# Attention scores of two maps, or of two heads, side by side in the upper and lower half of TensorE's array

## The chip, the cores and the metric

The kernel runs on one core of one Trainium2 chip. The metric is device time in microseconds (us) of one execution; of several runs the median counts. Durations of single instructions come from one profiled execution of the kernel, taken by the hardware profiler.

## The reference

An encoder trunk of two layers over 1024 tokens of width 1024, in float32. Each layer has a token mixer and an MLP with squared ReLU, both followed by a LayerNorm of the scaled residual. The mixer runs three groups beside each other: a convolution, differential attention (4 heads, with two score maps of 64 channels each) and attention to a memory of 256 rows (4 heads of 64 channels). What the change touches is this:

```python
# differential attention, per block of 128 queries and per head (dh = 64, S = 1024)
s1 = jnp.einsum("bhqd,bhkd->bhqk", q1b, k1).astype(jnp.float32) * scale + bias
s2 = jnp.einsum("bhqd,bhkd->bhqk", q2b, k2).astype(jnp.float32) * scale + bias
attn = jax.nn.softmax(s1, axis=-1) - lam * jax.nn.softmax(s2, axis=-1)
return jnp.einsum("bhqk,bhkd->bhqd", attn.astype(vh.dtype), vh)
...
# attention to the memory (MEM_DH = 64, 256 keys)
s = jnp.einsum("bshd,bmhd->bhsm", qh, km).astype(jnp.float32) * (MEM_DH ** -0.5)
p = jax.nn.softmax(s, axis=-1).astype(vm.dtype)
return jnp.einsum("bhsm,bmhd->bshd", p, vm).reshape(B, S, MEM_W)
```

## The kernel before

All large products run on TensorE in a float32 format of its own (`F32R` in the code). To keep precision each operand is split into a high and a low part (`split`), and a product is made of several: high x high, high x low and low x high, which is what `mm3` issues (L115 to L117).

A layer goes through stages: the input projection (`in_proj`, products `pj`, `v_ps`), the attention stage (`attention`), the output projection (`wo_ps`) with a LayerNorm, the MLP's upper product (`uz`, `uc`, `ud`) and its lower product (`db`, `dz`). The attention stage takes the heads in the order 0, memory (called head 4), 1, 2, 3, each in 8 blocks of 128 queries. A block passes through four steps in a software pipeline (`pipeline`):

- `scores`: TensorE makes the scores in PSUM; VectorE adds the bias, reduces to the row's extreme and writes to SBUF (L541); ScalarE takes the exponential (L543). For the memory it is a maximum (L551) and four exponentials (L555).
- `combine`: VectorE joins the two maps (L561 to L563), or the rows of the memory's heads are divided by their sums.
- `turn`: TensorE transposes the block (`at`, L199, 8 products of 128 columns), and it is split again by ScalarE with VectorE or with TensorE (L209).
- `values`: the products with the values (`o`, 24 of 256 columns for two blocks; `mo` for the memory), then the norm's small products (`ms`, L621 and L634).

A score has only 64 channels to sum over, and the array has 128 rows. For the differential heads the kernel stacks the high part of the queries on the low part (`qs`, 128 rows) and keeps the keys' high and low part twice, once in each half of the rows (`ks`, four slots). So a map of 128 queries by 512 keys takes two products of 128 rows (L538 with the keys' high parts, L539 with their low parts), and a block takes 8. For the memory two heads lie in the 128 rows of `qm`, and the keys `km` hold zeros where a row belongs to the other head, so one `mm3` makes both.

Scores go to a pool of two buffers of two PSUM banks each (`psum2`), one buffer per map. The memory's keys take the place of head 0's keys (`heads["k"]`, one buffer), and the load of a next head starts when the head before it begins (`before`, `load`). The order of the instructions on each engine is not the program's: a scheduler sorts them by priority when the program is built, and every engine then keeps that order.

Of the kernel before, what the change touches and what calls it, by code (L numbers as in the profile page):

```python
# [2 lines left out]

# [1 line left out]

# [7 lines left out]
F32R = mybir.dt.float32r  # L13
# [6 lines left out]
P = 128  # L20
T = 1024
# [4 lines left out]
MEM = 256  # L26
# [28 lines left out]
def encoder(ctx: ExitStack, tc: tile.TileContext, x, memt, w_f, w_v, w_mk, w_mv, w_out, w_up,  # L55
            w_down, par, lamv, bvr, emb_g, emb_b, rel, onehot, b_out, ln1_g, ln1_b, ln2_g, ln2_b, out):
    nc = tc.nc
# [6 lines left out]
    big = pool("big")  # L64
# [9 lines left out]
    def f(ap):  # L74
        return ap.bitcast(F32)
# [14 lines left out]
    def psum2(name):  # L90
        return pa.tile([P, 2, 512], F32, tag="pa", name=name)
# [14 lines left out]
    def weight(src, name, wpool=None, tag="w8", bufs=3, lo=None, hi=None):  # L106
        raw = wts.tile([P, 1024], F32, tag="raw", name=f"{name}_raw", bufs=3)
        loads.append(nc.sync.dma_start(raw, src))
        w = (wpool or wts).tile([P, 2, 1024], F32R, tag=tag, name=name, bufs=bufs)
        split(w[:, 0], w[:, 1], raw, lo or nc.gpsimd, hi)  # L110
        return w

    def mm3(ps, lhs, rhs, start, stop):

        nc.tensor.matmul(ps, lhsT=lhs[0], rhs=rhs[0], start=start, stop=False)  # L115
        nc.tensor.matmul(ps, lhsT=lhs[0], rhs=rhs[1], start=False, stop=False)  # L116
        nc.tensor.matmul(ps, lhsT=lhs[1], rhs=rhs[0], start=False, stop=stop)  # L117
# [367 lines left out]

    def attn_load(l, h, qd, kd, bt, qs, ks):
        nc.sync.dma_start(bt, skew[h][0:P * 2048].rearrange("(p n) -> p n", n=2048)[:, P - 1:P - 1 + BTW])
        for m in range(2):
            src = slice(64 * m, 64 * m + 64)
            for half in range(2):  # L490
                dst = slice(64 * half, 64 * half + 64)
                nc.sync.dma_start(f(ks[dst, 2 * m:2 * m + 2]), kd[src])
                nc.sync.dma_start(f(qs[dst, m]), qd[src, half])
        return ks, qs, bt

    def attention(l, heads, load, qmd, kvd, vt, lam, mixd, right):
# [10 lines left out]

        def out_w(kc, pr=None):
            wos[kc] = weight(w_out[l, kc * P:(kc + 1) * P, :], f"wo{l}_{kc}", *((pr, "wc", 5) if pr else ()), lo=nc.vector if kc in (4, 7) else None, hi=nc.gpsimd if kc in (1, 3, 5) else None)

        def scores(k):

            h, qb = k["h"], k["qb"]
            nm = f"{l}_{h}_{qb}"
            nonlocal ns
            if h == 0 and qb < 2:
                sc = wts.tile([P, 2, T], F32, tag="w8", name=f"s{nm}", bufs=3)
            elif h == NH and qb % 2:
                sc = k["prev"]["sc"][:, 1:2]
            elif ns % 3 == 0 and (h != NH - 1 or qb > 1):  # L520
                sc = heads["s"].tile([P, 2, T], F32, tag="s", name=f"s{nm}", bufs=1)
                ns += 1
            else:
                ns += 1
                sc = heads["b"].tile([P, 2, T], F32, tag="s", name=f"s{nm}", bufs=2)
            k["sc"] = sc
            if qb % 4 == 0 or (h == NH and qb % 2 == 0):
                sts[h, qb // 4] = sm.tile([P, 4, 8], F32, tag="ast", name=f"ast{nm}", bufs=3)
            st = k["st"] = sts[h, qb // 4][:, qb % 4]
            q = slice(qb * P, (qb + 1) * P)  # L530
            if h < NH:
                ks, qs, bt = heads[h]
                b0 = T - P - qb * P
                for m in range(2):
                    ps = psum2(f"sc{nm}_{m}")
                    for hf in range(2):
                        cs = slice(hf * 512, hf * 512 + 512)
                        nc.tensor.matmul(ps[:, hf], lhsT=qs[:, m, q], rhs=ks[:, 2 * m, cs], start=True, stop=False)  # L538
                        nc.tensor.matmul(ps[:, hf], lhsT=qs[:, m, q], rhs=ks[:, 2 * m + 1, cs], start=False, stop=True)  # L539

                    nc.vector.tensor_tensor_reduce(out=sc[:, m], in0=ps.rearrange("p a b -> p (a b)"), in1=bt[:, b0:b0 + T], scale=-0.125,  # L541
                                                   scalar=3e38, op0=ALU.add, op1=ALU.min, accum_out=st[:, m:m + 1])
                    nc.scalar.activation(sc[:, m], sc[:, m], AF.Exp, scale=-1.0, bias=st[:, m:m + 1], accum_out=st[:, 2 + m:3 + m])  # L543
            else:
                qm, km = heads[h], heads["km"]
                ps = psum2(f"sc{nm}")
                pv = ps.rearrange("p a (b m) -> p (a b) m", b=2)
                for c in range(2):
                    hs = slice(2 * c, 2 * c + 2)
                    mm3(ps[:, c], (qm[c][:, 0, q], qm[c][:, 1, q]), (km[:, 0, hs], km[:, 1, hs]), True, True)  # L550
                nc.vector.tensor_reduce(out=st[:, 0:4], in_=pv, op=ALU.max, axis=AX.X)  # L551
                nc.vector.tensor_scalar_mul(st[:, 0:4], st[:, 0:4], -0.125)
                p = sc[:, 0].rearrange("p (h m) -> p h m", h=NH)
                for i in range(NH):
                    nc.scalar.activation(p[:, i], pv[:, i], AF.Exp, scale=0.125, bias=st[:, i:i + 1], accum_out=st[:, 4 + i:5 + i])  # L555
# [32 lines left out]
        def values(k):  # L588

            h, qb, at = k["h"], k["qb"], k["at"]  # L590
            if h == NH:
                qc, vz = qb // 2, heads["vz"]
                pq = psum1(f"mo{l}_{qc}")
                for c in range(2):
                    for j in range(4):
                        i, mb = 2 * c + j // 2, j % 2
                        mm3(pq[:, 256 * c:256 * c + 256], (vz[:, 0, mb, i], vz[:, 1, mb, i]), (at[:, 0, 2 * i + mb], at[:, 1, 2 * i + mb]),
                            j == 0, j == 3)
                mx = wts.tile([P, 1024], F32, tag="raw", name=f"mmx{l}_{qc}", bufs=3)[:, 0:512]
                nc.scalar.activation(mx, pq, AF.Copy)  # L600
                for c in range(2):
                    store_mix(mx[:, 256 * c:256 * c + 256], mixd, 6 + c, 2 * qc, 2)
                return
# [4 lines left out]
            pq = po[h, qq]  # L608
# [125 lines left out]
    for l in range(L):  # L734
# [10 lines left out]
        def load(h):  # L745

            if h == 0:
                heads["k"] = heads["s"] = pool(f"k{l}", es=right, side="right")
            pr = heads["pool", h % 2]
            bt = pr.tile([P, BTW], F32, tag="bt", name=f"bt{l}_{h}", bufs=1)  # L750
            qs = pr.tile([P, 2, T], F32R, tag="qs", name=f"qs{l}_{h}", bufs=1)
            if h:
                ks = big.tile([P, 4, T], F32R, tag="b16", name=f"ks{l}_{h}", bufs=4)
            else:
                ks = heads["k"].tile([P, 4, T], F32R, tag="ks", name=f"ks{l}_{h}", bufs=1)
            heads[h] = attn_load(l, h, qd[h], kd[h], bt, qs, ks)

        heads["pool", 0] = pool(f"h{l}_0", es=right, side="right")
# [443 lines left out]
```

## Time and profile before

| | |
|---|---|
| median of 3 runs | 2441.92 us (2439.93 to 2450.11) |
| profiled execution | 2442.68 us |
| its span in the profile | 2440.8 us |
| granted TensorE clock, mean over the span | 0.987 |
| TensorE busy | 2320.9 us, 95% of the span |
| VectorE busy | 1769.6 us, 73% |
| ScalarE busy | 1174.7 us, 48% |

A busy time is the time in which at least one instruction of the engine is under way; matmuls overlap, so TensorE's busy time is not time at full rate. The attention stage lies at about 272 to 507 us in layer 0 and 1478 to 1701 us in layer 1. Names such as `sc<-ks,qs` say what is written and read, buffer numbers left out.

### The profile page before, as it was taken

The numbers are of one execution on the slowest core, as the hardware profiler recorded it, in microseconds if no ns is written. First come the engines' busy times: TensorE is split into PE (matmuls) and PEld (weight loads), VectorE is DVE, ScalarE is ACT, GpSimd is POOL, SyncE is SP. The second block draws the span as 40 slices with busy tenths as digits, with TensorE's granted clock in tenths as the row PEclk, the third lists the DMA queues.
The fourth block names the chain that finished last, engine by engine and source line by source line (L and its number), as shares of the span: only waits on it lengthen the run. The fifth ranks groups of instructions, "written<-read, shape, count | busy, mean of one in ns | idle before, by whom it ended". The sixth has DMA issues, their size and how long they took to land.

```text
span 2440.8 us, 30655 instructions
## 1 busy us (share of the span) xinstructions
PE 2320.9 (95%) x11516; PEld 1937.3 (79%) x11516; DVE 1769.6 (73%) x2516; ACT 1174.7 (48%) x2034; POOL 273.9 (11%) x184
## 2 busy tenths in 40 slices
PE   5999999999999998999999999999999999899997
PEld 4888788787788886888878887887878888688886
DVE  8697868847666657667789967786676566586768
ACT  5212488844655554333432227975465455433332
POOL 2224021111000000000033411111100000000002
PEclk9999999999999999999999999999999999999999
DMA  8252545241344458343332436434324444944332
GB/s 317 84 197 87 185 120 146 72 173 70 125 160 151 155 203 343 105 164 95 112 118 87 131 103 201 105 85 146 116 95 139 161 145 158 351 168 167 100 95 95
DMA packets 137740, 355.76 MB, mean 146 GB/s; under 512 B 14804, under 2 KB 31956, under 8 KB 130900
## 3 DMA queue, kind: packets, MB, share of 16 engines
q1 hardware_dynamic: 137592, 353.81, 43.3%
q8 instruction: 90, 1.47, 0.2%
q14 instruction: 58, 0.48, 0.1%
HBM read 240.47 MB, written 117.47 MB: 147 GB/s over the span
## 4 chain that ended last, share of the span: by engine, by line
PE 77%; DVE 16%; ACT 3%; DMA 3%; issue 2%; SPq 0%; DVEq 0%; ACTq 0%
PE uz L873 14%; PE db L1054 14%; PE dz L1054 10%; PE uc L873 7%; DVE acc L347 7%; PE ud L873 4%; PE wo_ps L117 2%; PE wo_ps L116 2%; PE wo_ps L115 2%; PE at L199 2%; DVE s L541 2%; PE pj L115 2%; PE pj L117 2%; PE pj L116 2%; PE sc L538 1%
## 5 line engine op out<-in xcount | busy, mean ns | idle before, releaser
L1054 PE MATMUL db<-wf,hf 128*128 128x512 f32 x1536 | 357.6, 392 | 22.7 <-ACT hf L99 21.6
L1054 PEld LDWEIGHTS db<-wf,hf 128*128 128x128 f32 x1536 | 289.5, 189 | 85.3 <-ACT hf L99 22.4
L1054 PE MATMUL dz<-wf,hf 128*128 128x512 f32 x1152 | 263.6, 389 | 0.0
L102 DVE TENSOR_TENSOR wf<-wd,wf 128x1024 fp32r<-128x1024 f32 x112 | 138.7, 1238 | 161.6 <-ACT wf L99 159.4
L1054 PEld LDWEIGHTS dz<-wf,hf 128*128 128x128 f32 x1152 | 216.7, 188 | 45.1
L99 ACT ACTIVATE wf<-wd 128x1024 fp32r<-128x1024 f32 x112 | 118.1, 1056 | 272.9 <-PE db L1054 132.4
L99 ACT ACTIVATE wu<-wu_r 128x512 fp32r<-128x512 f32 (+1 forms) x192 | 131.8, 708 | 219.8 <-PE uc L873 96.5
L873 PE MATMUL uz<-x,wu 128*128 128x512 f32 x768 | 191.5, 395 | 0.0
L873 PE MATMUL uz<-xt,wu 128*128 128x512 f32 x768 | 185.7, 389 | 1.0 <-ACT wu L99 1.0
L347 DVE SCALAR_TENSOR_TENSOR acc<-u,pp,acc 128x1009 f32<-128x1009 f32 (+14 forms) x120 | 185.4, 1585 | 0.6
L115 PE MATMUL pj<-x_h,wf 128*128 128x512 f32 x448 | 175.3, 392 | 1.7 <-ACT x_h L99 1.7
L116 PE MATMUL pj<-x_l,wf 128*128 128x512 f32 x448 | 175.1, 391 | 1.6 <-DVE l_row L126 1.6
L117 PE MATMUL pj<-x_h,wf 128*128 128x512 f32 x448 | 174.6, 390 | 0.0
L102 DVE TENSOR_TENSOR wu<-wu_r,wu 128x512 fp32r<-128x512 f32 (+1 forms) x192 | 145.9, 777 | 37.0 <-ACT wu L99 36.5
L873 PEld LDWEIGHTS uz<-x,wu 128*128 128x128 f32 x768 | 146.2, 191 | 31.2 <-ACT p L884 0.4
L873 PEld LDWEIGHTS uz<-xt,wu 128*128 128x128 f32 x768 | 143.9, 188 | 31.6 <-ACT wu L99 1.6
L541 DVE CUSTOM_DVE_ANT_0 s<-sc,bt 128x1024 f32<-128x1024 f32 x128 | 152.9, 1217 | 22.0 <-PE sc L539 15.6
L166 POOL TENSOR_TENSOR yd<-yd,l2g 128x1024 f32<-128x1024 f32 x6 | 17.2, 2870 | 1294.9 <-ACT yd L165 1294.9
L99 ACT ACTIVATE hf<-hr 128x1024 fp32r<-128x1024 f32 x112 | 117.3, 1049 | 93.9 <-PE db L1054 41.1
L543 ACT ACTIVATE s<-s,ast 128x1024 f32<-128x1024 f32 x128 | 148.4, 1164 | 26.8 <-DVE ast L541 26.4
L890 DVE TENSOR_TENSOR h<-u,uc 128x512 f32<-128x512 f32 x64 | 44.0, 687 | 135.2 <-PE uc L873 114.7
L102 DVE TENSOR_TENSOR hf<-hr,hf 128x1024 fp32r<-128x1024 f32 x112 | 137.0, 1223 | 4.1 <-ACT hf L99 4.1
(261 smaller groups left out, 5082.8 us busy)
## 6 DMA issues: line engine op xcount, KB each, us to landing
hr<-hd SPq DMA_DIRECT2D x224, 256.0 KB, 2.9
wu_r<-in_w_up SPq DMA_DIRECT2D x64, 512.0 KB, 4.1
hd<-hs SPq DMA_DIRECT2D x128, 256.0 KB, 2.9
wd<-in_w_down SPq DMA_DIRECT2D x64, 512.0 KB, 7.3
hd<-h SPq DMA_DIRECT2D x96, 256.0 KB, 2.1
ks<-kd SPq DMA_DIRECT2D x32, 512.0 KB, 9.8
wf_raw<-in_w_f SPq DMA_DIRECT2D x28, 512.0 KB, 4.2
qd<-stg SPq DMA_DIRECT2D x8, 1024.0 KB, 4.3
```

The lines of the kernel that those rows point to most:

```text
L99: nc.scalar.activation(hi, src, AF.Copy)
L102: (lo_eng or nc.vector).tensor_tensor(lo, src, f(hi), op=ALU.subtract)
L115: nc.tensor.matmul(ps, lhsT=lhs[0], rhs=rhs[0], start=start, stop=False)
L116: nc.tensor.matmul(ps, lhsT=lhs[0], rhs=rhs[1], start=False, stop=False)
L117: nc.tensor.matmul(ps, lhsT=lhs[1], rhs=rhs[0], start=False, stop=stop)
L199: nc.tensor.matmul(pt[:, j * P:(j + 1) * P], lhsT=src, rhs=ident, start=j == 0, stop=j == 3, is_transpose=True, skip_group_check=True)
L347: nc.vector.scalar_tensor_tensor(acc[:, c, a:b], u[:, c, a + t - PAD:b + t - PAD], pp[:, k:k + 1], acc[:, c, a:b], ALU.mult, ALU.add)
L541: nc.vector.tensor_tensor_reduce(out=sc[:, m], in0=ps.rearrange("p a b -> p (a b)"), in1=bt[:, b0:b0 + T], scale=-0.125, scalar=3e38, op0= ...
L543: nc.scalar.activation(sc[:, m], sc[:, m], AF.Exp, scale=-1.0, bias=st[:, m:m + 1], accum_out=st[:, 2 + m:3 + m])
L873: nc.tensor.matmul(ps, lhsT=a[:, kc], rhs=x[:, c, kc], start=start and kc == 0 and n == 0, stop=stop and kc == 3 and n == 2, skip_group_ch ...
L890: nc.vector.tensor_tensor(h, a, ps, op=op)
L1054: nc.tensor.matmul(ps, lhsT=h[:, a, n, ts], rhs=w[c][:, n], start=start and n == 0 and m == 0, stop=stop and n == 1 and m == 2, skip_group ...
```

## The change

The scores of a head's two maps are now made side by side: map 0 in rows 0 to 63 of the array, map 1 in rows 64 to 127, in the places in which `qd` and `kd` hold them. A map takes three products of 64 rows (high x high, high x low, low x high) for each half of the keys, and the new function `halves` issues one of map 1 and one of map 0 in turn, into the two buffers of the block. It also ties each such product behind the one before it on TensorE, and gives all but the first of a block another priority in the scheduler. The memory's heads are made in pairs in the same way, with 256 columns each, and their order in the banks changes with it. Queries and keys are loaded with one transfer each.

```diff
@@ -1,5 +1,5 @@
 import math
-from contextlib import ExitStack
+from contextlib import ExitStack, nullcontext
 
 import numpy as np
 
@@ -485,12 +485,8 @@
 
     def attn_load(l, h, qd, kd, bt, qs, ks):
         nc.sync.dma_start(bt, skew[h][0:P * 2048].rearrange("(p n) -> p n", n=2048)[:, P - 1:P - 1 + BTW])
-        for m in range(2):
-            src = slice(64 * m, 64 * m + 64)
-            for half in range(2):
-                dst = slice(64 * half, 64 * half + 64)
-                nc.sync.dma_start(f(ks[dst, 2 * m:2 * m + 2]), kd[src])
-                nc.sync.dma_start(f(qs[dst, m]), qd[src, half])
+        nc.sync.dma_start(f(ks), kd)
+        nc.sync.dma_start(f(qs), qd)
         return ks, qs, bt
 
     def attention(l, heads, load, qmd, kvd, vt, lam, mixd, right):
@@ -507,6 +503,18 @@
 
         def out_w(kc, pr=None):
             wos[kc] = weight(w_out[l, kc * P:(kc + 1) * P, :], f"wo{l}_{kc}", *((pr, "wc", 5) if pr else ()), lo=nc.vector if kc in (4, 7) else None, hi=nc.gpsimd if kc in (1, 3, 5) else None)
+
+        pairs = []
+
+        def halves(outs, lhs, rhs, start=True, stop=True):
+
+            for n, (a, c) in enumerate(((0, 0), (0, 1), (1, 0))):
+                for m in (1, 0):
+                    r = slice(64 * m, 64 * m + 64)
+
+                    with (tc.issue_after(pairs[-1].ins) if pairs else nullcontext()), tc.high_priority(offset=0 if start and n == 0 and m else 400):
+                        pairs.append(nc.tensor.matmul(outs[m], lhsT=lhs[m][a][r], rhs=rhs[m][c][r], start=start and n == 0,
+                                                      stop=stop and n == 2, skip_group_check=True))
 
         def scores(k):
 
@@ -531,12 +539,11 @@
             if h < NH:
                 ks, qs, bt = heads[h]
                 b0 = T - P - qb * P
-                for m in range(2):
-                    ps = psum2(f"sc{nm}_{m}")
-                    for hf in range(2):
-                        cs = slice(hf * 512, hf * 512 + 512)
-                        nc.tensor.matmul(ps[:, hf], lhsT=qs[:, m, q], rhs=ks[:, 2 * m, cs], start=True, stop=False)
-                        nc.tensor.matmul(ps[:, hf], lhsT=qs[:, m, q], rhs=ks[:, 2 * m + 1, cs], start=False, stop=True)
+                pm = [psum2(f"sc{nm}_{m}") for m in range(2)]
+                for hf in range(2):
+                    cs = slice(hf * 512, hf * 512 + 512)
+                    halves([pm[m][:, hf] for m in range(2)], [(qs[:, 0, q], qs[:, 1, q])] * 2, [(ks[:, 0, cs], ks[:, 1, cs])] * 2)
+                for m, ps in enumerate(pm):
 
                     nc.vector.tensor_tensor_reduce(out=sc[:, m], in0=ps.rearrange("p a b -> p (a b)"), in1=bt[:, b0:b0 + T], scale=-0.125,
                                                    scalar=3e38, op0=ALU.add, op1=ALU.min, accum_out=st[:, m:m + 1])
@@ -545,9 +552,10 @@
                 qm, km = heads[h], heads["km"]
                 ps = psum2(f"sc{nm}")
                 pv = ps.rearrange("p a (b m) -> p (a b) m", b=2)
+
                 for c in range(2):
-                    hs = slice(2 * c, 2 * c + 2)
-                    mm3(ps[:, c], (qm[c][:, 0, q], qm[c][:, 1, q]), (km[:, 0, hs], km[:, 1, hs]), True, True)
+                    halves([ps[:, i, c * MEM:(c + 1) * MEM] for i in range(2)], [(qm[c][:, 0, q], qm[c][:, 1, q])] * 2,
+                           [(km[:, 0, 2 * c + i], km[:, 1, 2 * c + i]) for i in range(2)], c == 0, c == 1)
                 nc.vector.tensor_reduce(out=st[:, 0:4], in_=pv, op=ALU.max, axis=AX.X)
                 nc.vector.tensor_scalar_mul(st[:, 0:4], st[:, 0:4], -0.125)
                 p = sc[:, 0].rearrange("p (h m) -> p h m", h=NH)
@@ -593,8 +601,8 @@
                 pq = psum1(f"mo{l}_{qc}")
                 for c in range(2):
                     for j in range(4):
-                        i, mb = 2 * c + j // 2, j % 2
-                        mm3(pq[:, 256 * c:256 * c + 256], (vz[:, 0, mb, i], vz[:, 1, mb, i]), (at[:, 0, 2 * i + mb], at[:, 1, 2 * i + mb]),
+                        i, o, mb = 2 * c + j // 2, c + j // 2 * 2, j % 2
+                        mm3(pq[:, 256 * c:256 * c + 256], (vz[:, 0, mb, i], vz[:, 1, mb, i]), (at[:, 0, 2 * o + mb], at[:, 1, 2 * o + mb]),
                             j == 0, j == 3)
                 mx = wts.tile([P, 1024], F32, tag="raw", name=f"mmx{l}_{qc}", bufs=3)[:, 0:512]
                 nc.scalar.activation(mx, pq, AF.Copy)
@@ -750,9 +758,9 @@
             bt = pr.tile([P, BTW], F32, tag="bt", name=f"bt{l}_{h}", bufs=1)
             qs = pr.tile([P, 2, T], F32R, tag="qs", name=f"qs{l}_{h}", bufs=1)
             if h:
-                ks = big.tile([P, 4, T], F32R, tag="b16", name=f"ks{l}_{h}", bufs=4)
+                ks = big.tile([P, 4, T], F32R, tag="b16", name=f"ks{l}_{h}", bufs=4)[:, 0:2]
             else:
-                ks = heads["k"].tile([P, 4, T], F32R, tag="ks", name=f"ks{l}_{h}", bufs=1)
+                ks = heads["k"].tile([P, 4, T], F32R, tag="ks", name=f"ks{l}_{h}", bufs=1)[:, 0:2]
             heads[h] = attn_load(l, h, qd[h], kd[h], bt, qs, ks)
 
         heads["pool", 0] = pool(f"h{l}_0", es=right, side="right")
```

The first place is TensorE's order at block 3 of head 2. Before (`sc_2_3_0` and `sc_2_3_1` are the block's two maps):

```order
L538 MATMUL sc_2_3_0_3668<-ks_2_3063,qs_2_3062 128x512
L539 MATMUL sc_2_3_0_3668<-ks_2_3063,qs_2_3062 128x512
L538 MATMUL sc_2_3_0_3668<-ks_2_3063,qs_2_3062 128x512
L539 MATMUL sc_2_3_0_3668<-ks_2_3063,qs_2_3062 128x512
L538 MATMUL sc_2_3_1_3675<-ks_2_3063,qs_2_3062 128x512
L539 MATMUL sc_2_3_1_3675<-ks_2_3063,qs_2_3062 128x512
L538 MATMUL sc_2_3_1_3675<-ks_2_3063,qs_2_3062 128x512
L539 MATMUL sc_2_3_1_3675<-ks_2_3063,qs_2_3062 128x512
L199 MATMUL at_2_0_0_3567<-ident,s_2_0_3488 128x128 x4
```

Now, the last three pairs of the same block and what follows:

```order
L516 MATMUL sc_2_3_1_3769<-ks_2_3131,qs_2_3130 128x512
L516 MATMUL sc_2_3_0_3768<-ks_2_3131,qs_2_3130 128x512
L516 MATMUL sc_2_3_1_3769<-ks_2_3131,qs_2_3130 128x512
L516 MATMUL sc_2_3_0_3768<-ks_2_3131,qs_2_3130 128x512
L516 MATMUL sc_2_3_1_3769<-ks_2_3131,qs_2_3130 128x512
L516 MATMUL sc_2_3_0_3768<-ks_2_3131,qs_2_3130 128x512
L209 MATMUL at_2_1_0_3705<-at_2_0_3662,minus 128x512
L209 MATMUL at_2_1_1_3713<-at_2_0_3662,minus 128x512
```

The block's products stay together in both. There were four for map 0 and then four for map 1; now all twelve alternate between the maps, and both maps end with the last pair.

The second place is TensorE's order between head 0's last scores (`sc_0_7`) and the memory's first (`sc_4_0`). Before, the end of that piece:

```order
L116 MATMUL o_0_0_2467<-at_0_2_2416,v_6_671 128x256
L117 MATMUL o_0_0_2467<-at_0_2_2416,v_6_671 128x256
L115 MATMUL o_0_0_2467<-at_0_2_2416,v_7_672 128x256
L116 MATMUL o_0_0_2467<-at_0_2_2416,v_7_672 128x256
L117 MATMUL o_0_0_2467<-at_0_2_2416,v_7_672 128x256
L199 MATMUL at_0_5_1_2552<-ident,s_0_5_2492 128x128 x4
L209 MATMUL at_0_4_1_2518<-at_0_4_2510,minus 128x512
L209 MATMUL at_0_5_0_2544<-at_0_4_2510,minus 128x512
L621 MATMUL ms_0_0_2587<-ones,rms_0_2328 128x1 x4
```

Now, from the last pair of head 0 on:

```order
L516 MATMUL sc_0_7_1_2630<-ks_0_2044,qs_0_2043 128x512
L516 MATMUL sc_0_7_0_2629<-ks_0_2044,qs_0_2043 128x512
L209 MATMUL at_0_5_0_2566<-at_0_4_2528,minus 128x512
L209 MATMUL at_0_5_1_2574<-at_0_4_2528,minus 128x512
L629 MATMUL ms_0_0_2609<-ones,rms_0_2326 128x1 x4
L199 MATMUL at_0_6_0_2651<-ident,s_0_6_2544 128x128 x4
L199 MATMUL at_0_6_1_2658<-ident,s_0_6_2544 128x128 x4
L209 MATMUL at_0_6_1_2658<-at_0_6_2650,minus 128x512
L516 MATMUL sc_4_0_2674<-kv_2323,qm_2320 128x256 x12
```

Before, 11 value products of head 0 (`o`) and two groups of four transpositions (`at`, L199) stood in this piece. Now no value product stands here: they come after the memory's first scores, and eight transpositions and a third L209 fill the place.

The third place is the beginning of block 4 of head 1 now:

```order
L199 MATMUL at_1_2_1_3338<-ident,s_1_2_3241 128x128 x4
L516 MATMUL sc_1_4_1_3349<-ks_1_2668,qs_1_2667 128x512
L209 MATMUL at_1_2_1_3338<-at_1_2_3330,minus 128x512
L516 MATMUL sc_1_4_0_3348<-ks_1_2668,qs_1_2667 128x512
L516 MATMUL sc_1_4_1_3349<-ks_1_2668,qs_1_2667 128x512
L516 MATMUL sc_1_4_0_3348<-ks_1_2668,qs_1_2667 128x512
```

The first product of the block stands alone, with one of L209 behind it, and the others follow in turn. That is so for 30 blocks; in all, TensorE's order now has 106 stretches of paired products, with 960 products where there were 608.

## Rows read from the trace of the kernel before

**Rows 1.** The profile page, part 1: busy us (share of the span), instructions
```profile
PE 2320.9 (95%) x11516; PEld 1937.3 (79%) x11516; DVE 1769.6 (73%) x2516; ACT 1174.7 (48%) x2034; POOL 273.9 (11%) x184
```

**Rows 2.** Stretches: length, PE, PEld, DVE, ACT, POOL busy us, granted clock, DMA
```profile
272.00:507.00 235.00, 220.97 (x1353) 187.63 (x1352) 181.30 (x336) 181.74 (x379) 36.55 (x42) 0.97 0.43 122
1478.00:1701.00 223.00, 208.78 (x1315) 180.28 (x1314) 166.42 (x315) 172.92 (x365) 38.84 (x43) 0.98 0.44 123
```

**Rows 3.** Chain of waits inside the same two stretches, shares
```profile
by line: PE at L199 10.6%; DVE s L541 9.5%; PE sc L538 7.9%; PE sc L539 7.3%; PE o L115 5.6%; PE o L116 5.5%; PE o L117 5.5%; PE at L209 4.2%; DVE s L563 3.2%; issue 3.1%; ACT s L555 3.0%; PE ms L634 2.3%; ACT at L208 2.2%; DMA kv<-kvd 2.0%
...
by line: PE at L199 11.4%; DVE s L541 9.5%; PE sc L538 7.8%; PE sc L539 7.4%; PE o L115 6.6%; PE o L116 6.5%; PE o L117 6.5%; PE at L209 4.5%; DVE s L563 3.5%; PE ms L634 2.8%; DMA kv<-kvd 2.2%; issue 2.2%; PE wo_ps L116 2.1%; PE wo_ps L115
```

**Rows 4.** Groups by line and shape, TensorE: count, busy us, mean ns, idle
```profile
L538 PE MATMUL sc<-ks,qs 128*128 128x512 f32 x256 | 108.6, 424 | 14.8 <-DVE ast L541 13.0 <-PE sc L539 0.9 <-ACT s L555 0.4
L539 PE MATMUL sc<-ks,qs 128*128 128x512 f32 x256 | 103.1, 403 | 0.0
...
L115 PE MATMUL sc<-kv,qm 128*128 128x512 f32 x32 | 14.3, 447 | 3.1 <-DMA kv<-kvd 1.6 <-ACT s L555 1.4
...
L116 PE MATMUL sc<-kv,qm 128*128 128x512 f32 x32 | 13.1, 410 | 0.0
```

**Rows 5.** Timeline of TensorE, a block of head 1: start us, length us, instruction
```profile
372.47 0.39 PE L538 MATMUL sc<-ks,qs 128*128 128x512 f32 x1
372.70 0.39 PE L539 MATMUL sc<-ks,qs 128*128 128x512 f32 x1
372.92 0.39 PE L538 MATMUL sc<-ks,qs 128*128 128x512 f32 x1
373.15 0.39 PE L539 MATMUL sc<-ks,qs 128*128 128x512 f32 x1
373.38 1.91 PE L199 MATMUL at<-ident,s 128*128 128x128 f32 x16
```

**Rows 6.** Timeline of TensorE, transpositions and then value products
```profile
308.02 1.09 PE L199 MATMUL at<-ident,s 128*128 128x128 f32 x8
308.87 0.37 PE L115 MATMUL o<-at,v 128*128 128x256 f32 x1
309.07 0.28 PE L116 MATMUL o<-at,v 128*128 128x256 f32 x1
309.19 0.28 PE L117 MATMUL o<-at,v 128*128 128x256 f32 x1
```

**Rows 7.** Busy time by stretch, around the memory's scores of layer 0
```profile
316.00:326.00 10.00, 8.80 (x46) 7.23 (x45) 6.92 (x17) 5.92 (x13) 0.00 (x0) 0.83 0.82 295
340.00:360.00 20.00, 19.15 (x123) 16.06 (x122) 10.27 (x23) 18.41 (x59) 9.28 (x20) 1.00 0.13 38
```

**Rows 8.** Who waited for the products that read ks (us, times)
```profile
who waited for it (us, times):
  DVE s L541: 15.6, 15
```

**Rows 9.** The profile page, part 5: the reduction of a map's scores
```profile
L541 DVE CUSTOM_DVE_ANT_0 s<-sc,bt 128x1024 f32<-128x1024 f32 x128 | 152.9, 1217 | 22.0 <-PE sc L539 15.6
```

**Rows 10.** Chain of waits in order of time, layer 0 (start us, us)
```profile
316.74 4.75 DMA kv<-kvd
```

**Rows 11.** Timeline of TensorE, up to the memory's first scores
```profile
320.28 1.05 PE L621 MATMUL ms<-ones,rms 128*128 128x1 f32 x8 [0.91 <-ACT om L618]
321.62 0.76 PE L115 MATMUL sc<-kv,qm 128*128 128x512 f32 x1 [0.29 <-DMA kv<-kvd]
322.19 0.63 PE L116 MATMUL sc<-kv,qm 128*128 128x512 f32 x1
322.61 0.63 PE L117 MATMUL sc<-kv,qm 128*128 128x512 f32 x1
```

**Rows 12.** The profile page, part 6: KB each, us from issue to landing
```profile
ks<-kd SPq DMA_DIRECT2D x32, 512.0 KB, 9.8
```

**Rows 13.** Timeline of TensorE's weight loads, same block of head 1
```profile
376.05 0.19 PEld L539 LDWEIGHTS sc<-ks,qs 128*128 128x128 f32 x1
```

## The prediction

> **What bounds the kernel now.** I read the engines' totals first. TensorE holds matmuls for 95% of the span, VectorE and ScalarE much less [rows 1]. The change touches only the attention stage of each layer, so the rest is read there. In the two stretches that hold it, 235 and 223 us long, TensorE is busy 221 and 209 us, VectorE 181 and 166, ScalarE 182 and 173 [rows 2]: TensorE leads, the other two are not far behind. The chain of waits inside those stretches says the same in shares: the score products (L538 and L539) hold 15.2% of it in both layers, that is 35.7 and 33.9 us, VectorE's reduction of the scores (L541) another 9.5% [rows 3]. So score products count when they get shorter, but not all of them.
>
> How many are there? 256 and 256 of 512 columns for the four differential heads, and 3 x 32 for the memory's heads (L115 to L117, the third is like the second) [rows 4]. Their listed length (about 0.4 us) is not their price, for they overlap. The price is the distance between starts: 372.47, 372.70, 372.92, 373.15, 373.38, so 0.2275 us [rows 5]. That makes 512 x 0.2275 = 116.5 us for the heads (58.2 per layer) and 96 x 0.2275 = 21.8 us for the memory. Of the 116.5 us the chain holds 35.7 + 33.9 = 69.6, a share of 0.6. I take this 0.6 as what the end feels of a microsecond of TensorE there.
>
> **The scores of the heads.** Before, a block (128 queries of one head) issues 8 products of 128 rows: two maps, two halves of the keys, two products. Now it issues 12 of 64 rows, always one of map 1 and then one of map 0. No product of 64 rows with such a partner is in the trace, so a pair is bounded: at best it takes the time of one product, 0.2275 us; at worst its two run in turn, 0.455 us. Each product also has its own weight load. The nearest row for their rate are the transpositions, where load and product come in turn with 128 columns each: 8 from 308.02 to 308.87, 0.106 us each [rows 6]. Two loads take 0.21 us and still fit beneath 0.2275. I take full overlap: the two halves of a pair read different partitions and write different banks, and nothing in a row speaks against it. Then 2 layers x 4 heads x 8 blocks = 64 blocks, x 6 pairs = 384 pairs x 0.2275 = 87.4 us, 29.1 less than 116.5. With the share of 0.6: -17.5 us. The point from which it turns: 8 x 0.2275 = 6 pairs x 0.303, so a pair must stay under 0.303 us.
>
> The Trainium skill, page "TensorE: Matmul & The Clock Gate", Part 3 (packing small matmuls), gives 3.07 times for four products of 32 rows side by side, and a model by which partners start 4 ns apart. No run here shows it yet. An estimate from that 3.07 of a possible 4 would give a pair 0.2275 x 2 / 1.53 = 0.297 us, 114 us in all, and hardly any gain; from the 4 ns it would be the 87.4 above.
>
> **The memory's scores.** 96 products of 512 columns become 96 pairs of 256. A product of 256 columns starts 0.12 us after the one before [rows 6], so 11.4 us at best; at the rate of two loads per pair (0.21) 20.2 us; in turn (0.24) 23. That is -10 to +1 against 21.8. I take the loads' rate, being the nearest row, with some of it overlapped: -5 on TensorE, and -3 at the end, since ScalarE holds 18.4 of 20 us in that part [rows 7].
>
> **What is added.** A block's two maps used to be finished one after the other: VectorE could begin after 4 products (0.91 us) while TensorE made the second map. Now both end together after 6 pairs, 1.37 us, so the first reduction can begin 0.46 us later, the second 0.45 us earlier, and the next block's first pair needs both buffers back. VectorE waited for the last score product 15 times, 15.6 us in all [rows 8]; 15 x 0.46 = 7 us is the upper bound, below nothing if the earlier second map counts (-7). I take +2.5: between two reductions of 1.22 us [rows 9] most starts are late anyway.
>
> In the new order 30 of a block's first products stand alone, ahead of another instruction. Each breaks the pairing by one place: at most 30 x 0.2275 = 6.8 us of TensorE, nothing where it fills a wait. I take +2.
>
> The memory's keys are loaded into the place of head 0's keys, so the load waits for head 0's last score. It is on the chain with 4.75 us in layer 0 [rows 10], and then TensorE, whose granted clock is 0.83 over these 10 us, takes 0.42 to 0.43 us per product: it has fallen to the 1.2 GHz level behind waits of 0.91 and 0.29 us [rows 7, 11]. In the old order 3.0 us of work stand between that last score and the memory's first (4 + 4 transpositions, 11 value products, two L209, 4 of L621); in the new order 1.9 us (8, none, three, 4), and the value products come behind. That is 1.1 us more of waiting per layer and perhaps a longer slow stretch: 0 to +5, I take +2.
>
> **What costs nothing.** Per head 8 transfers become 2 of 1 MB, and half of the keys' bytes go. No wait of TensorE names them; they landed in 9.8 us [rows 12] during the head before. If that cover were gone it would now be shorter, not longer. VectorE's and ScalarE's instructions keep their number and shapes. The memory's value products only read other columns.
>
> Sum: -17.5 - 3 + 2.5 + 2 + 2 = -14 us. The profiled execution took 2442.7 us, so 2428.7; the median of the runs lies 0.8 below it, which gives 2428.
>
> **The rivals.**
> *The pairs run in turn* (slower). Then the heads take 768 x 0.2275 = 174.7 us, 58 more, and the memory 1 more. At the share of 0.6 that is +35, and since TensorE with 221 of 235 us has no room it goes towards +58: 2478 to 2501, say 2488. The deciding point is the 0.303 us above. For it: no row shows two products at once, their starts are always 0.23 or 0.12 apart. Against it: each alone fills only half the rows of the array.
>
> *Each change between products of 128 and of 64 rows costs time.* The new order has 106 stretches of paired products, so 212 changes. A product lasts 0.39 us and the next starts after 0.23 [rows 5]; if the next had to wait for the end, 0.16 us would go each time: 34 us, which eats the 29. With the weight load (0.19 us, [rows 13]) uncovered too it is 0.35 us, 74 us: +45 - 5 on TensorE, +24 at the end, 2467. So 2443 to 2467. Against it: between score products and transpositions, two kinds already mixed, the distance stays 0.23 [rows 5], so the nearest row says nothing is lost. The skill speaks for it: "TensorEngine Tiling (Array Packing)", Tiling Modes, says that changing the tiling mode drains TensorE. The trace has no such change in this stage.
>
> *The overlap works, but VectorE and ScalarE hold the stage.* Both are busy 77% of it [rows 2], and a block needs both reductions done before its successor begins. Then at most a third of the 17.5 + 3 us reaches the end and the rest comes back as waits: 2436 to 2443, say 2439.
>
> **How the numbers follow.** This kernel's runs tell a change of 0.5%, 12 us, from none. Forecast: 0.57, own range 2410 to 2437. Its low end has a share of 0.8 (0.8 x 29 = 23) and 8 for the memory, -31; its high end all added costs near their bounds, -17.5 - 0.5 + 5 + 4 + 4 = -5. I give three quarters of it to times below 2429.7, since each of the three added costs may be nothing. Pairs in turn: 0.17. Price of the change of shape: 0.14, half of it within 0.5%. VectorE and ScalarE: 0.12, nearly all no change. Faster: 0.43 + 0.04 = 0.47 (0.04 from the best ends of the last two). Same: 0.14 + 0.06 + 0.09 = 0.29. Slower: 0.17 + 0.07 = 0.24. The range 2410 to 2462 leaves out the pairs in turn and the very ends.
>
> **What would show it.** In the new profile the starts of paired products should come in twos within some ns, a pair every 0.23 us. A distance of 0.23 between all starts would be the pairs in turn. A gap of 0.16 or more at the beginning and end of each stretch of pairs would be the price of the change of shape. If the pairs run at 0.23 and TensorE's waits for L541 grow from 13 us [rows 4] by ten or more, VectorE and ScalarE hold the stage. The attention stretches should shrink to about 228 and 216 us, while all others keep their length; if they move too, something else happened.

## The result and the profile after

The changed kernel took 2502.18 us (median of 4 runs, 2494.45 to 2504.64), the kernel before 2442.73 us beside it (4 runs). The ratio is 1.0234, with a 95% interval of 1.0208 to 1.0259: 59.5 us slower. The forecast was 2428, 14.7 us faster, and the range ended at 2462. The profiled execution took 2494.45 us, span 2492.7, mean granted clock 0.975.

The totals, which answer to [rows 1]:

```profile
PE 2351.7 (94%) x11868; PEld 1937.3 (78%) x11868; DVE 1775.2 (71%) x2516; ACT 1177.6 (47%) x2034; POOL 270.0 (11%) x184
```

The two attention stretches, each from the first score to the first product of the output projection (columns as in [rows 2], whose stretches were cut a little differently). First before, layers 0 and 1, then after:

```profile
272.41:501.74 229.33, 215.30 (x1327) 182.85 (x1326) 180.86 (x336) 180.61 (x376) 36.55 (x42) 0.98 0.41 116
1456.18:1685.56 229.38, 213.78 (x1327) 183.24 (x1326) 181.47 (x336) 179.32 (x375) 35.17 (x42) 0.97 0.42 117
```

```profile
272.36:528.51 256.15, 229.66 (x1502) 183.30 (x1502) 183.09 (x336) 182.20 (x376) 34.68 (x42) 0.92 0.27 92
1483.67:1737.51 253.84, 229.18 (x1502) 182.08 (x1502) 182.67 (x336) 181.76 (x376) 35.16 (x42) 0.92 0.27 93
```

The loss lies here: the stretches were 229.3 and 229.4 us long and are 256.2 and 253.8, and every other stage keeps its length to within 1 us. VectorE and ScalarE do the same work in a longer stretch (183.1 and 182.2 us in layer 0), so they wait longer. Of TensorE's 26.8 us more in layer 0, only 12.5 are idle time (14.0 before, 26.5 now); the other 14.4 are busy time, at a granted clock of 0.92 instead of 0.98. Both have to be explained.

TensorE's timeline at the beginning of head 0 shows how the pairs run (start, length, instruction, count of those put together, idle time before). The line at 290.59 is from a narrow window inside the twelve products, and shows the second pair alone:

```profile
289.94 0.39 PE L117 MATMUL pj<-x_h,wf 128*128 128x512 f32 x1
290.25 1.66 PE L516 MATMUL sc<-ks,qs 64*128 64x512 f32 x12
...
290.59 0.39 PE L516 MATMUL sc<-ks,qs 64*128 64x512 f32 x2
...
291.84 1.09 PE L199 MATMUL at<-ident,s 128*128 128x128 f32 x8
293.33 0.50 PE L516 MATMUL sc<-ks,qs 64*128 64x512 f32 x1 [0.40 <-DVE ast L548]
293.76 0.49 PE L209 MATMUL at<-at,minus 128*128 128x512 f32 x1
294.48 1.66 PE L516 MATMUL sc<-ks,qs 64*128 64x512 f32 x11 [0.22 <-DVE ast L548]
```

Twelve products take 291.84 - 290.25 = 1.59 us until the transposition behind them starts. The two products of the second pair together last no longer than one (0.39 us): the pairs do run side by side. Six pairs at 0.23 are 1.38, and 0.21 is left over: 0.11 lies between the first pair and the second (290.25 to 290.59), the other 0.10 behind the last pair. Entering costs as well: the stretch starts 0.31 us after the L117 product, where 0.2275 is usual [rows 5], so about 0.08. A lone first product puts the next instruction 0.43 us behind it (293.33 to 293.76). The granted clock is 1.00 in these places, so this is not the lower clock. A block without a lone product therefore takes 0.08 + 1.38 + 0.21 = 1.67 us, against 8 x 0.2275 = 1.82 before.

So at the full clock TensorE's own part is no loss. The chain of waits in the stretch 272 to 528, by line, tells where the time went; compare [rows 3]:

```profile
by line: PE sc L516 14.7%; ACT s L550 13.4%; PE at L199 9.2%; DVE s L571 6.0%; issue 5.1%; DVE s L548 4.6%; PE at L209 4.2%; PE o L115 4.1%; PE o L116 4.1%; PE o L117 4.0%; ACT at L208 3.5%; DVE ast L570 2.9%; ACT at L210 2.9%; ACT s L563 2
```

The exponential of a map (L550, L543 before) does not stand among the lines shown of before; now it holds 13.4%, 34 us. The join of the two maps (L571, L563 before) went from 3.2% to 6.0%. The heads' scores held 15.2%, all scores together hold 14.7% now.

VectorE's waits over the whole run say the same. First before (its waits for scores are in [rows 8]), then after (who waits, for whom: us, times, longest):

```profile
DVE ast L561 <- ACT s L543: 19.1, 18, 2.4
```

```profile
DVE ast L570 <- ACT s L550: 54.6, 47, 2.4
DVE s L548 <- PE sc L516: 19.2, 23, 2.4
DVE ast L569 <- ACT s L550: 12.4, 33, 1.5
```

Waits for the scores grew by 3.6 us only; waits of the join for the exponential grew from 19 to 54.6 + 12.4 = 67. One place shows the mechanism whole, on VectorE, ScalarE and TensorE in turn (timelines of head 1, blocks 3 and 4):

```profile
388.00 1.23 DVE L548 CUSTOM_DVE_ANT_0 s<-sc,bt 128x1024 f32<-128x1024 f32 x1 [0.85 <-PE sc L516]
...
389.14 1.22 DVE L548 CUSTOM_DVE_ANT_0 s<-sc,bt 128x1024 f32<-128x1024 f32 x1
...
391.10 0.16 DVE L569 RECIPROCAL ast<-ast 128x1 f32<-128x1 f32 x1
392.72 0.22 DVE L570 SCALAR_TENSOR_TENSOR ast<-ast,lam 128x1 f32<-128x1 f32 x1 [1.45 <-ACT s L550]
392.97 1.28 DVE L571 SCALAR_TENSOR_TENSOR s<-s,ast 128x1024 f32<-128x1024 f32 x1
...
394.25 1.22 DVE L548 CUSTOM_DVE_ANT_0 s<-sc,bt 128x1024 f32<-128x1024 f32 x1
```

```profile
389.83 1.15 ACT L550 ACTIVATE s<-s,ast 128x1024 f32<-128x1024 f32 x1
...
391.44 1.15 ACT L550 ACTIVATE s<-s,ast 128x1024 f32<-128x1024 f32 x1
```

```profile
390.43 1.65 PE L516 MATMUL sc<-ks,qs 64*128 64x512 f32 x11
394.31 1.09 PE L199 MATMUL at<-ident,s 128*128 128x128 f32 x8 [2.23 <-DVE s L571]
```

Both reductions of block 3 are done at 390.4. Next in VectorE's order stands that same block's join, which needs the exponentials of both maps. ScalarE ends the second at 391.44 + 1.15 = 392.59, so VectorE stands still for 1.45 us. Block 4's scores are complete at 390.43 + 1.65 = 392.08 and their reductions could run, but VectorE works in order: they start at 394.25, after the join. TensorE, whose two score buffers are full and whose next transpositions need the join, stands still for 2.23 us. Before, it went like this at such a place (the order of VectorE around block 3 of head 2; L541 lines are the reductions of maps, L563 the join):

```
L541 ISA s_2_3_3667,ast_2_0_3489<-sc_2_3_0_3668,bt_2_3061 128x1024
...
L541 ISA s_2_3_3667,ast_2_0_3489<-sc_2_3_1_3675,bt_2_3061 128x1024
...
L541 ISA s_2_4_3706,ast_2_4_3707<-sc_2_4_0_3708,bt_2_3061 128x1024
...
L541 ISA s_2_4_3706,ast_2_4_3707<-sc_2_4_1_3715,bt_2_3061 128x1024
...
L563 SCALAR_TENSOR_TENSOR s_2_3_3667<-s_2_3_3667,ast_2_0_3489 128x1024
```

and in the changed kernel, around block 4 of head 1:

```
L548 ISA s_1_4_3346,ast_1_4_3347<-sc_1_4_1_3349,bt_1_2666 128x1024
...
L548 ISA s_1_4_3346,ast_1_4_3347<-sc_1_4_0_3348,bt_1_2666 128x1024
...
L569 RECIPROCAL ast_1_4_3347<-ast_1_4_3347 128x1
L570 SCALAR_TENSOR_TENSOR ast_1_4_3347<-ast_1_4_3347,lam_651 128x1
L571 SCALAR_TENSOR_TENSOR s_1_4_3346<-s_1_4_3346,ast_1_4_3347 128x1024
L548 ISA s_1_5_3410,ast_1_4_3347<-sc_1_5_1_3412,bt_1_2666 128x1024
```

Call a join early if no reduction of a later block stands between it and its own block's. Before, 26 of the 64 joins are early; now 52 are. No line of VectorE was touched: the scheduler placed the joins anew when the products changed.

The pauses reach the clock too. Behind a wait of 1.86 us for a join (the transposition at 297.99) it is granted at 0.67 over 10 us of head 0, so TensorE spends most of them at the 1.2 GHz level:

```profile
300.00:310.00 10.00, 8.31 (x33) 5.09 (x34) 5.94 (x14) 6.50 (x12) 0.00 (x0) 0.67 0.35 148
```

Over a stretch, (1 - clock) x 2 x length gives the time at the lower level: 0.08 x 2 x 256 = 41 us in layer 0, against 0.02 x 2 x 229 = 9 before. Work done there takes up to twice its time, so the difference can make up to 16 us of busy time: about as much as TensorE's busy time grew (14.4).

### The profile page after: what moved, and what is told of

Read it like the earlier page. It is cut to its first block, busy times and chain, and to the rows that moved or that the text cites. A ratio compares the mean times of both kernels' runs of the same rounds, so it can differ in the third digit from the quotient of the medians.

```text
span 2492.7 us, 31341 instructions
## 1 busy us (share of the span) xinstructions
PE 2351.7 (94%) x11868; PEld 1937.3 (78%) x11868; DVE 1775.2 (71%) x2516; ACT 1177.6 (47%) x2034; POOL 270.0 (11%) x184
## 4 chain that ended last, share of the span: by engine, by line
PE 75%; DVE 14%; ACT 7%; issue 2%; DMA 2%; SPq 0%; DVEq 0%; ACTq 0%
PE uz L881 14%; PE db L1062 13%; PE dz L1062 10%; PE uc L881 7%; DVE acc L347 7%; PE ud L881 3%; PE sc L516 3%; PE wo_ps L117 2%; PE wo_ps L115 2%; PE wo_ps L116 2%; ACT s L550 2%; PE at L199 2%; PE pj L115 2%; PE pj L116 2%; PE pj L117 2%
## 5 line engine op out<-in xcount | busy, mean ns | idle before, releaser
L117 PE MATMUL pj<-x_h,wf 128*128 128x512 f32 x448 | 175.7, 393 | 0.0
L550 ACT ACTIVATE s<-s,ast 128x1024 f32<-128x1024 f32 x128 | 147.0, 1150 | 46.7 <-DVE ast L548 46.4
L516 PE MATMUL sc<-ks,qs 64*128 64x512 f32 x768 | 141.2, 448 | 14.2 <-DVE ast L548 10.9
```

The source lines that it names most:

```text
L516: pairs.append(nc.tensor.matmul(outs[m], lhsT=lhs[m][a][r], rhs=rhs[m][c][r], start=start and n == 0, stop=stop and n == 2, skip_group_che ...
```

## The experiments

Ratios are against the kernel before, run beside it on the same chip, with 95% intervals; differences are of medians. The code is shortened: names before a call and conditions for a first product are left out. An edit that ties or moves something lets the scheduler place the rest anew, so these runs do not change one engine's order alone.

**First: pairs, or the order around them?** e1 keeps the products of 128 rows, but chains them as the changed kernel chains its pairs (same priorities, maps in turn, both buffers asked for at once). e2 keeps the pairs, but makes them from the two key halves of one map, so that the maps end one after the other. e3 and e4 do one part each.

```diff
 e1: for hf in range(2): for n in range(2): for m in (1, 0):
+        with issue_after(pairs[-1]), high_priority(offset=0 if n == 0 and m else 400):
+            matmul(pm[m][:, hf], lhsT=qs[:, m, q], rhs=ks[:, 2 * m + n, cs], ...)
 e2: for m in range(2):
+        ps = psum2(f"sc{nm}_{m}")
+        halves([ps[:, hf] for hf in range(2)], [(qs[:, 2 * m, q], qs[:, 2 * m + 1, q])] * 2, [(ks[:, 2 * m], ks[:, 2 * m + 1])] * 2)
 e3: the memory's scores as before     e4: the heads' scores as before
```

> The products of the kernel before (128 rows, 8 per block, 0.2275 us each, two whole copies of the keys), but issued as the change issues its pairs: the maps in turn, both ended by the last product, each tied behind the one before, first of a block at its own priority. No pair, no change of array shape. Theory A (both maps end together, so VectorE starts late and TensorE needs both buffers back before it can begin the next block): it is slower than the kernel before by most of the 52 to 60 us, say +35 to +60. Theory B (the change of array shape, 0.30 us per stretch as the trace of the changed kernel shows, and the low clock behind it): within 10 us of the kernel before.

e1: 2469.65 us, ratio 1.0096 (1.006 to 1.0132), +26 us. With no 64-row product, nearly half of the loss is there, between the two ranges expected. VectorE's waits for the last score product doubled (15.6 before), and the joins' waits for the exponential, 16.5 and another 9.5, are above the 19.1 of before (30 early joins):

```profile
DVE s L546 <- PE sc L542: 29.8, 32, 3.8
DVE ast L567 <- ACT s L548: 16.5, 17, 2.4
```

> Pairs kept, but a pair is now the two halves of the keys of ONE map (queries of the map in both halves of the rows, keys 0 to 511 in the upper half, 512 to 1023 in the lower), so a map ends after three pairs (0.68 us) and its buffer alone is needed for the next map; the memory's part is as in the change. Stretches of 64-row products: 102 against 106, so the price for the array's shape stays. Theory A: the loss goes and the shorter products show, 2425 to 2450 us. Theory B: the loss stays, 2485 to 2505 us.

e2: 2454.29 us, 1.0036 (1.0019 to 1.0053), +11 us, with 28 early joins, a little above the range for "the loss goes". Pairs alone are no loss of that size, but no gain either.

> The change for the four differential heads alone; the memory's scores and values as before. Both theories: nearly the whole loss, +45 to +60 us, since 64 of the 80 blocks are here. If it is below +30, the memory's pairs cost more than their share.

e3: 2494.45 us, 1.0203 (1.0168 to 1.0238), +51 us: the heads' part carries the loss.

> The change for the memory's heads alone; the differential heads as before. A memory block uses one buffer for all its heads in both kernels, so theory A expects no loss, -10 to +3 us. Theory B expects 16 blocks x 0.30 us against 10 us of shorter products: -5 to +5. Both: within 0.5% of the kernel before.

e4: 2441.25 us over 10 runs, 0.9984 (0.9968 to 0.9999), -2 us. The memory's pairs give back hardly more than the measurement can tell.

**Second: the price of a change of shape, and of the order.** e5 is the kernel before with the low-part products on rows 0 to 63 alone, which leaves out low x low; 128-row and 64-row products alternate then. e6 is e1 with map after map, and map 0's products first. e7 and e8 are the changed kernel and e2 without the priority.

```diff
 e5:
-nc.tensor.matmul(ps[:, hf], lhsT=qs[:, m, q], rhs=ks[:, 2 * m + 1, cs], start=False, stop=True)
+nc.tensor.matmul(ps[:, hf], lhsT=qs[0:64, m, q], rhs=ks[0:64, 2 * m + 1, cs], start=False, stop=True)
 e6: e1's two lines, in the loops
+for m in range(2): for hf in range(2): for n in range(2):
 e7, e8:
-with issue_after(pairs[-1]), tc.high_priority(offset=0 if start and n == 0 and m else 400):
+with issue_after(pairs[-1]):
```

> The kernel before, with one edit: the second product of each map and half (low parts of the keys) uses rows 0 to 63 alone, so it leaves out low x low; columns, buffers, order of the maps and transfers as before, no pairs. 256 single products of 64 rows stand between products of 128 rows. Theory B with the price read in the changed kernel's trace (0.09 us on entering, 0.21 us on leaving): 256 x 0.29 = 75 us on TensorE, at the end +45 to +75 us. If a change of the array's shape costs nothing: -2 to +5 us.

e5: 2562.98 us, 1.0491 (1.0454 to 1.0529), +120 us, more than was expected at most. TensorE's timeline of a block, to be compared with [rows 5]:

```profile
395.41 0.40 PE L538 MATMUL sc<-ks,qs 128*128 128x512 f32 x1
395.74 0.50 PE L539 MATMUL sc<-ks,qs 64*128 64x512 f32 x1
396.17 0.50 PE L538 MATMUL sc<-ks,qs 128*128 128x512 f32 x1
396.60 0.49 PE L539 MATMUL sc<-ks,qs 64*128 64x512 f32 x1
...
398.31 0.50 PE L539 MATMUL sc<-ks,qs 64*128 64x512 f32 x1
398.75 0.44 PE L199 MATMUL at<-ident,s 128*128 128x128 f32 x2
```

Starts lie 0.43 us apart, not 0.2275: each change of the number of rows costs 0.20 us, the first of a block 0.10. At the lower clock products would start as far apart (0.42 to 0.43 us, [rows 11]), but from 395 to 399 us the granted clock is 1.00. With this block taken for all 64, 64 x (7 x 0.20 + 0.10) = 96 us of the 120. The rule of the Trainium skill that spoke against this change ("TensorEngine Tiling (Array Packing)", Tiling Modes, Key Properties: a switch of the mode drains TensorE) agrees with this row; it has no price.

> Control for the run with the maps in turn (+26 us): the same 128-row products, the same chain and priority and both buffers asked for at once in the program, but map 0's four products first and then map 1's four. Theory A (both maps end together): within 8 us of the kernel before. If the chain and the priority did it by moving the other work: again +15 to +30 us.

e6: 2454.13 us, 1.0044 (1.0028 to 1.006), +11 us. Chain, priority and asking for both buffers at once cost this much, a little more than was expected (29 early joins). It is also e2's partner, since it has the same order of maps without pairs: 2454.13 against 2454.29, although e2 has the memory's pairs besides. Pairs bring nothing net.

> The changed kernel without its priority (chain kept). If the lone first products (30 of them) and what the priority moves matter: 10 us or more off its 2500. Theory A with B: they are a small part, 2490 to 2510 us.

e7: 2511.1 us, 1.0282 (1.0266 to 1.0298), +68 us, just above what was expected (53 joins early). The priority is not the cause. (In the changed kernel's code the first product of each half of the keys is the exception to the other priority, so two products of a block and not one.)

> Pairs of the two halves of one map's keys (run at 2454 us), without the priority. 131 stretches instead of 102, so by the price of 0.30 us 9 us more on TensorE: 2455 to 2465 us by theory B; if the order matters more than the number of stretches it may fall below 2450.

e8: 2458.73 us, 1.0065 (1.0047 to 1.0083), +16 us. It has 131 stretches of pairs where e2 has 102, but also 17 early joins instead of 28, and the two intervals overlap, so it gives no price of a stretch.

**Third: VectorE's order.** e9 to e12 are the changed kernel, the kernel before, e2 and e1, with each join called later in the program and tied behind the next block's reductions (60 joins are late in e9 to e12; four, ahead of the memory and at the end of each layer, have no such block behind them).

```diff
+with tc.issue_after(nxt["red"].ins):   # the last reduction of the next block
     nc.vector.reciprocal(st[:, 4:5], st[:, 3:4])
...
```

> The changed kernel, but VectorE's joining of a block's two maps is tied behind both reductions of the next block (60 of 64 blocks; in the changed kernel's own order 52 of 64 joins stand right behind their block's reductions, where VectorE waits for ScalarE's exponential, 27 + 7 us per layer). Theory C (the order on VectorE makes most of the loss): 2445 to 2470 us. Theory A with B alone (both maps end together, price of the array's shape): the loss stays, 2485 to 2505 us.

e9: 2474.5 us, 1.0122 (1.0104 to 1.014), +29 us: 28 us of the loss are gone when the joins move; a few us less than hoped. TensorE's order moved with them (in layer 0 its stretch holds 1490 products, not 1502), but the 106 stretches of pairs stay. The join no longer waits for the exponential, the reductions wait more for scores:

```profile
DVE s L548 <- PE sc L516: 41.6, 27, 2.8
...
DVE ast L570 <- ACT s L550: 3.9, 4, 1.2
```

> Control: the kernel before with the same late joining. 26 of its joins stood right behind their reductions, VectorE waited 8 us per layer for the exponential there. Theory C: equal or a little faster, 2428 to 2445 us. If the late joining is itself worth tens of us, it would show here too.

e10: 2457.71 us, 1.0057 (1.0041 to 1.0073), +12 us. A miss: late joins do not help the kernel before, they cost it. Late is not good in itself; the mixture of before was better than either.

> Pairs of the two halves of one map's keys (2454 us, 28 joins right behind their reductions, 18 us per layer of waiting) with the late joining. Theory C: 10 to 20 us less, 2434 to 2446. Theory B: TensorE bound with nothing won, 2448 to 2456.

e11: 2458.84 us, 1.006 (1.0045 to 1.0075), +14 us. A miss as well: in this kernel too late joins gain nothing (e2 had +11). It lies 1 us from e10, but e10 lacks the chain and the priority, so this says nothing clean about the pairs.

> The 128-row products with the maps in turn (2470 us; 30 joins right behind their reductions) with the late joining. Theory A: the loss stays, 2462 to 2475, since both maps still end together and both buffers are still needed. Theory C: it goes down to 2445 to 2455.

e12: 2478.43 us, 1.0141 (1.0114 to 1.0168), +33 us. Above both ranges: the loss of the maps that end together stays with late joins. e9, the same with pairs, is 4 us faster, within the intervals.

**Fourth: the loss without a pair.** If early joins are the cause, they must slow the kernels that have no pairs. e13 is e1 and e14 is the kernel before, with all 64 joins early.

```diff
+with tc.issue_after(joins[-1].ins):    # the join of the block before
     nc.vector.tensor_tensor_reduce(out=sc[:, m], ...)
```

> No pair and no change of array shape: 128-row products with the maps in turn (2470 us), and VectorE's first reduction of each block tied behind the joining of the block before, so that all 64 joins stand right behind their own reductions (52 in the changed kernel, 30 in the run at 2470). Theory A with C (the maps end together, and VectorE waits for the exponential): the loss of the changed kernel appears without its pairs, 2490 to 2515 us. If the pairs or their shape made the rest of it: 2468 to 2480 us.

e13: 2515.56 us, 1.0291 (1.0257 to 1.0325), +72 us, as much as expected at most, without one product of 64 rows:

```profile
DVE ast L570 <- ACT s L551: 51.5, 35, 2.9
DVE ast L569 <- ACT s L551: 43.1, 53, 2.6
```

> The kernel before with the same order of the joins (64 right behind their reductions instead of 26), map after map as always. Theory C alone: +20 to +40 us. If the order hurts only where both maps end together: +0 to +12 us.

e14: 2495.91 us, 1.0207 (1.0185 to 1.0229), +53 us, more than the +20 to +40 expected, with the products of before and none of them tied on TensorE. (The scheduler moved some all the same: 1303 products stand in the stretch, 1327 did before.) Its attention stretch has nearly the changed kernel's length and the same clock, and VectorE's waits have the same cause:

```profile
272.39:525.76 253.37, 220.81 (x1303) 190.56 (x1301) 183.11 (x336) 181.51 (x375) 35.95 (x42) 0.92 0.36 105
```

```profile
DVE ast L564 <- ACT s L546: 87.8, 58, 2.8
```

## Why the prediction was wrong

**The overlap: right.** A pair takes 0.23 us, as forecast, and even the memory's pair of 256 columns does better than the loads' rate that was taken: twelve products in 0.92 us (340.67 to 341.59), with 0.21 over as in the heads, so about 0.12 per pair. The rival of pairs in turn gave 2488, near the result, but is refuted: that it came near is luck. The Trainium skill ("TensorE: Matmul & The Clock Gate", Part 3) says partners start within some ns; the second pair shown above, two products in 0.39 us, agrees. The estimate of 0.297 us from its factor of 3.07 does not hold here.

**The change of shape: mis-sized, the rival's mechanism was right.** It was taken at nothing, because transpositions and score products mix freely; but both of these use all 128 rows, so that row did not bear on it. Measured it is 0.08 + 0.11 + 0.10 = 0.29 us for the stretch shown, where the rival had 2 x 0.16; 106 like it would make 31 us of TensorE. The savings forecast for TensorE were 29.1 us for the heads and, with pairs of 0.12, some 10 for the memory. What is left, 8 us x 0.6, is 5 us, and the two comparisons with the same chain gave 0 (e2 with e6) and -4 (e9 with e12). So this step turned -20.5 into about nothing, but does not make the kernel slower.

**Both maps ending together: right mechanism, too small.** The forecast was +2.5 with a bound of 7. From e6 to e1, the same chain with maps in turn instead of one after the other, it is +15 us. The bound counted only the waits that were there before, 15 of them; e1 has 32. Whether the late start or the need for both buffers at once weighs more was not separated.

**"VectorE's and ScalarE's instructions keep their number and shapes": the step that failed.** That sentence is true, and the price of nothing does not follow from it. Their order changed: 26 early joins became 52. e9 takes 28 us off the changed kernel by moving the joins back. From the other side, e14 makes 38 more joins early for +53 us and e13 34 more for +46 over e1, about 1.4 us per join; the changed kernel has 22 more than e1, about 30 us. This price holds only for joins made early beyond the order of before: making them late there gained nothing (e10, e11, e12). The third rival, by which VectorE and ScalarE hold the stage, named the right engines, but let them only eat the gain, since their busy time does not grow. It missed that an engine busy 71% of the time can set the end by waiting in order. Its sign was the wrong wait as well: TensorE's waits for the reductions went from 13 us to 10.9, while its transpositions' waits for the join went from 0.5 to 10.4:

```profile
PE at L199 <- DVE s L563: 0.5, 2, 0.3
...
PE sc L516 <- DVE ast L548: 10.9, 22, 0.9
PE at L199 <- DVE s L571: 10.4, 9, 2.2
```

**The parts together.** Chain, priority and buffers +11 (e6), maps together +15 (e1 over e6), pairs with their changes of shape about 0 (-4 to 0), early joins +28 to +30: 50 to 56 of the 59.5 us. What remains is about the width of these intervals. Each part holds what it costs through the clock. That the parts add up is assumed, for they were measured in different kernels; the first two also hold what the scheduler moved along.

**The rest.** The gap from the start of head 0's last score product to the memory's first went from 5.3 us (316.32 to 321.62) to 5.8 (325.91 to 331.75) in layer 0, and from 5.5 to 5.3 in layer 1: less than the 1.1 per layer that was forecast. No wait of TensorE names the load there any more; it waits 1.58 us for ScalarE's part of a transposition. Lone first products cost 0.43 each instead of nothing to 0.2275; they end a stretch of their own, and are among the 106. That loads and stages outside the attention would not move was right.

**What stays open.** Why the scheduler put the joins early: only its outcome was seen. What the lower clock costs by itself: at 41 against 9 us at the 1.2 GHz level it is up to (41 - 9) / 2 = 16 us of TensorE per layer, which could be more than half of the loss. The runs show that it comes and goes with the waits (0.92 in e14 too, 0.95 in e9), but none held the waits and changed the clock. No version was faster than the kernel before by more than the 2 us of e4.

## What to carry to other kernels

When a scheduler places the instructions, compare the order on every engine behind the edit, not only on the one that is edited; an instruction that waits for another engine and stands ahead of ready work costs both. Halves of the array pay only in long stretches: here a block of 12 saves 0.44 us by pairing and pays 0.29 for entering and leaving. And a consumer that takes results one at a time is best served one at a time: finishing two maps together cost 15 us here, more than the pairs saved.

## What was unexpected about the hardware

Going from a product of 128 rows to one of 64, or back, delays the next start by 0.20 us (0.43 instead of 0.2275 us, at a granted clock of 1.00 in e5's timeline). A stretch of pairs pays 0.08 on entering, 0.11 between its first pair and the second and 0.10 on leaving. Two products of 64 rows in different halves overlap fully, at 0.23 us a pair with 512 columns and about 0.12 with 256, each with its own weight load.
